# Projections into four PSUM banks until a layer's first scores, and gate projection z:0 moved ahead of the first merge

## The chip, the cores and the metric

One core of a Trainium2 chip runs the whole program. Its engines are PE (matmul; PEld loads its weights), DVE (vector), ACT (scalar functions), POOL (GpSimd) and SP, which here only issues transfers. The metric is the device time of one execution in microseconds, lower is better.

## The reference

Two decoder layers on a sequence of 256 with width 1024, in float32. Cut to what matters here:

```python
proj = x @ w_in                       # q, k, v of both mixers, gate z, decay logits
q_a, k_a, v_a, a_logit, b_logit, z, q_b, k_b, v_b = jnp.split(proj, offs, -1)
# group A: gated DeltaNet, 4 heads of 128, chunks of 64
qkv = jax.nn.silu(causal_dwconv(jnp.concatenate([q, k, v], -1), conv_w))   # width 4
sol = lax.linalg.triangular_solve(t_mat, rhs, left_side=True, lower=True, unit_diagonal=True)
o = o * lax.rsqrt(jnp.mean(o * o, -1, keepdims=True) + NORM_EPS) * norm_g
o = o * jax.nn.silu(z)
# group B: causal softmax attention with partial rotary on q and k, 8 heads of 64
mix = jnp.concatenate([o_a, o_b], -1) @ w_out
x = layer_norm(DEEPNORM_ALPHA * x + mix, ln1_g, ln1_b)
hid = causal_dwconv(x @ w_up, ffn_conv_w) + ffn_conv_b                     # width 3
ffn = (jax.nn.silu(gate) * val) @ w_down
x = layer_norm(DEEPNORM_ALPHA * x + ffn, ln2_g, ln2_b)
```

With 256 positions and blocks of 256 the block-sparse attention is plain causal attention.

## The kernel before

**Projections.** Activations lie transposed, 128 channels by 256 positions a tile. `proj` makes one projection of 128 channels: SP loads a weight chunk into `wr` (L181; ring of 6), ACT rounds it to a high part `wh` (L196) and DVE takes the residue `wl` (L197; on some chunks of the feed-forward part POOL does), both in rings of 5, and PE runs 24 matmuls: eight pairs for high weights with the high and low part of the input (L211, L212), then eight for the residues (L214). The result stands in one PSUM bank, which is read from there: a convolution unit (`ka`, `va`, `qa`) has ACT scale it into `cv` (L424), DVE add three shifted products (L427, each reading the bank), ACT take tanh (L429) and DVE the product (L430); a gate unit (`z`) has ACT take tanh (L441) and DVE the product (L442); a rotary unit (`qb`, `kb`) has ACT copy it (L447) and DVE shuffle and multiply (L449, L450).

**PSUM.** Eight banks: two called `pj` (projections), two called `mx` (scores, their transposes, products with the values and the last steps of the DeltaNet group), four called `ac` (small matrices, later the output projection). A tile taken from a group waits until the tile that held its bank before has been read for the last time.

**Mixer of a layer.** The DeltaNet group builds a matrix per head (`kk`, `decay`, `am`), writes it to DRAM, and POOL inverts its blocks of 16 (`solve`, L527 to L530). The inverse goes to DRAM (L531) and comes back spread over the partitions (L538). Unit `ex` expands it on DVE (L543), and the merges `lt` (L560), `lx` (L575, L581), `mt` (L596) and `mx` (L605, L607) join blocks to 32, 64 and 128. Here the "first merge" begins with `ex`. `zsol`, `az` and `o` apply it (L691, L697, L703), DVE normalizes the outputs (L711), and `ot` transposes them (L719). The attention group runs for each pair of heads `s` (scores L619 and mask L623 on PE, maximum L625 and L626 on DVE, exponential L633 on ACT), `tr` (transposes, L648 to L650) and `pv` (L662, L663). Each `s` and each `tr` takes both `mx` banks. `w` units begin the output projection (L732 to L734).

**Order.** `ORDER` lists the units of a layer. A unit's instructions are traced in that order, and a scheduler then places them on each engine, with priority by the order traced; an instruction may be placed earlier than its unit where its inputs are there in the scheduler's own model. Letters behind `@` forbid that: the unit's instructions on that engine (P for PE, A, D, G for POOL) stay behind the last ones of the unit before. At run time each engine follows its fixed order and waits on semaphores.

Of the kernel before, what the change touches and what calls it, by code (L numbers as in the profile page):

```python
# [22 lines left out]
D = 1024  # L23
S = 256
# [12 lines left out]
DP = 8 * (NB * 128 + NB)  # L37
# [33 lines left out]

ORDER = ("""
ab ka:0@A ab2@G ka:2@P qb:0@GP ka:3@G ka:1 kk:0 decay@AGD kk:1@PG kb:0@G kb:2@G sk@GP ld:0@P ld:1@DG kb:3@G am:0@A
vb:1@DAGP qb:1@GP kb:1@G rp@DG am:1@AG qb:2@G qb:3 va:2@GP va:0@G va:3 rk@G solve@G va:1@D qa:1 qa:0@P ex@DPA lt@GP s:0@DA lx@DAP
tr:0@AD mt:32:0@GAP mx:32:0@G mt:32:1@G vt:0@G rp@GP mx:32:1@PAG pv:0 mt:64:0@GDPA mt:64:1@AG s:1@AGD
qa:3@G qa:2@GP mx:64:0@PG tr:1@PA mx:64:1@D z:0 s:2@GADP pv:1@GA sq:0@DG vt:1@ADP zsol:0@D az tr:2@A s:3@GDP pv:2@AG
tr:3@PGD zsol:1@A z:2@G qk@GP sq:1@GDA o:0@ADP z:1@G wu:1@PGA pv:3@AGP o:1@GDP w:0:5 w:0:4@D w:1:4@PDA z:3@PD w:1:6@G
w:0:7@GD w:1:5@GPD ot:1@AP ot:0@G wu:0@PA w:0:6@A
""", """
vb:1@APDG ab@GD ka:0@G ab2@G ka:3 qb:0@P ka:2@G ka:1@P kk:0 decay@ADG kb:0 kk:1@GA kb:2 sk@AP kb:3@G kb:1@PG qb:2  # L80
rp@GPD qb:3@GP am:0@PA qb:1@DP am:1@AG ld:0@GP va:1@P va:0@GP rk@AG va:2@G ld:1@D solve@GP va:3@P qa:1 ex@D lt@DAP s:0@GD
lx@DAPG mt:32:0@A mt:32:1@AG vt:0@PD rp@GAD tr:0@AP qa:0 mx:32:0 pv:0@A mx:32:1@AD mt:64:0@AGD mt:64:1@DGP s:1@A
qa:3 qa:2@P mx:64:1@APD tr:1@P z:0@G s:2@G sq:0@D vt:1@DG mx:64:0@GDP pv:1 zsol:0@DGP az@A tr:2@DA s:3@GD pv:2@AG
tr:3@PDGA zsol:1@PD z:2 qk@PDG sq:1@G o:0@ADP z:1 pv:3@AGD o:1@A w:0:5@G w:0:4@DP w:1:4@GDA z:3@PA wu:0@DP w:1:6@GP
wu:1@GA w:0:7@D ot:1@D ot:0@AP w:1:5 w:0:6@PA
""")
# [3 lines left out]
def hybrid_kernel(ctx, tc, xT, x, wab, wch, par, lnrow, cst, msk, out):  # L90
# [22 lines left out]
    def ps_p():  # L113
        return ps_w()[:, 0:S]
# [4 lines left out]
    def ps_m():  # L119
        return mx.tile([128, 512], F32, name="mx")  # L120
# [217 lines left out]
    vb = vb_first()  # L338
    const_prep()

    for l in range(DEPTH):
# [79 lines left out]
        def gdn_conv(ps, ct, dst):  # L421
# [7 lines left out]
            act.activation(th, cv, AF.Tanh, scale=0.5)  # L429
            dve.scalar_tensor_tensor(dst, th, 1.0, cv, op0=OP.add, op1=OP.mult)  # L430

        def u_conv(c0, ct, dst, h):
            ps = ps_p()
            proj(ps, l, c0 + h)
            gdn_conv(ps, ct + h, dst[:, h, :])

        def u_z(h):
            ps = ps_p()
            proj(ps, l, C_Z + h)
            th = mt("th", [128, S], 2)  # L440
            act.activation(th, ps, AF.Tanh, scale=0.5)  # L441
            dve.scalar_tensor_tensor(zs[:, h, :], th, 1.0, ps, op0=OP.add, op1=OP.mult)  # L442

        def u_rope(c0, dst, p):
            ps = ps_p()
            proj(ps, l, c0 + p)
            act.activation(dst[:, p, :], ps, AF.Copy)  # L447
            sw = mt("sw", [128, S], N_SW)
            dve.stream_shuffle(sw, dst[:, p, :], [(i + 8) % 16 if i < 16 else i for i in range(32)])  # L449
            dve.tensor_tensor(dst[:, p, :], dst[:, p, :], ropec, op=OP.mult)  # L450
            st["rp"] = st.get("rp", []) + [(dst, p, sw)]
# [158 lines left out]
                    dve.tensor_copy(X[hi, b, :, 0:n], ps[hi])  # L610

        def u_s(p):
            sc = [ps_m() for _ in range(2)]
            mxv = small.tile([128, 4], F32, name="mxv")
            for js, ks in ((slice(0, 128), slice(0, 128)), (slice(128, 384), slice(0, S))):
                for a in range(2):
                    rs = slice(64 * a, 64 * a + 64)
                    qs = slice(js.start, js.start + 128)
                    pe.matmul(sc[a][:, js], qb[rs, p, qs], kb[rs, p, ks], start=js.start == 0, stop=False,  # L619
                              skip_group_check=True)  # L620
            for a in range(2):
                for i in (0, 256):
                    pe.matmul(sc[a][:, i:i + 128], ident_b, neg_lt, start=False, stop=i > 0, skip_group_check=True)  # L623
            for a in range(2):
                dve.tensor_reduce(mxv[:, a:a + 1], sc[a][:, 0:128], axis=AX.X, op=OP.max)  # L625
                dve.tensor_reduce(mxv[:, 2 + a:3 + a], sc[a][:, 128:384], axis=AX.X, op=OP.max)  # L626
            dve.tensor_scalar(mxv, mxv, -(DH ** -0.5), None, op0=OP.mult)
            P = [mt("P0", [128, 2, 128], 2), mt("P1", [128, 2, S], 2)]
            sv = small.tile([128, 4], F32, name="sv")
            for i, js in enumerate((slice(0, 128), slice(128, 384))):  # L630
                for a in range(2):
                    c = 2 * i + a
                    act.activation(P[i][:, a, :], sc[a][:, js], AF.Exp, scale=DH ** -0.5, bias=mxv[:, c:c + 1],  # L633
                                   accum_out=sv[:, c:c + 1])
            rv = small.tile([128, 4], F32, name="rv")
            dve.reciprocal(rv, sv)
            for i in range(2):
                for a in range(2):
                    c = 2 * i + a
                    dve.tensor_scalar(P[i][:, a, :], P[i][:, a, :], rv[:, c:c + 1], None, op0=OP.mult)  # L640
            st["P", p] = P
# [362 lines left out]
```

## Time and profile before

| | |
|---|---|
| three runs | 713.30, 714.86, 716.22 us; median 714.86 |
| profiled execution | 714.04 us, of which the span from first to last instruction is 712.3 |
| mean granted clock of PE | 0.984 |
| busy share of the span | PE 97%, DVE 81%, ACT 56%, POOL 28% |
| mixer of layer 0, of layer 1 | about 19 to 161 us, 367 to 512 us |

Busy time of PE counts pipelined matmuls from start to modelled end, so that short waits between them do not show. The granted clock is a share of 2.4 GHz; 0.50 is 1.2 GHz. Idle time of an engine is put down to the event that ended it.

### The profile page before, as it was taken

To read this page: it belongs to the slowest core of one execution; us is meant where nothing else is said; L and a number is where in the kernel's file an instruction comes from. 1 tells how busy PE (TensorE), PEld (TensorE's weight loads), DVE (VectorE), ACT (ScalarE), POOL (GpSimd) and SP (SyncE) were. 2 spreads that over 40 slices of the span, in tenths; PEclk is the share of its full clock that TensorE was granted. 3 is DMA by queue.
4 is the path that set the end of the run, shared out by engine and by line. 5 is a ranking of instruction groups with operands and counts; after the bars stand their busy time and mean duration, and the time that the engine had idled before them with its cause. 6 is when DMAs were issued, how large, how long until landed. Compare 5 with 4: busy or idle time off the path is not lost.

```text
span 712.3 us, 13664 instructions
## 1 busy us (share of the span) xinstructions
PE 688.6 (97%) x5056; PEld 618.6 (87%) x5056; DVE 576.9 (81%) x1273; ACT 400.8 (56%) x908; POOL 197.2 (28%) x200
## 2 busy tenths in 40 slices
PE   8989999999999999999999989999999999999994
PEld 5979888787999999999888988888789999999994
DVE  5899877599788887778879987776998888887756
ACT  5644466546666665656355445556476566666531
POOL 0045700013333343332002382000153333333413
PEclk9999999999999999999999997999999999999998
DMA  8876351521766665656153437134246766666201
GB/s 313 305 244 192 78 198 40 199 89 61 276 220 194 211 222 184 202 181 205 60 201 129 144 94 222 61 103 159 66 150 234 233 213 194 214 206 202 70 1 60
DMA packets 41217, 118.07 MB, mean 166 GB/s; under 512 B 10176, under 2 KB 12992, under 8 KB 40640
## 3 DMA queue, kind: packets, MB, share of 16 engines
q1 hardware_dynamic: 41152, 117.21, 49.6%
q8 instruction: 40, 0.66, 0.3%
q14 instruction: 25, 0.20, 0.1%
HBM read 114.84 MB, written 2.36 MB: 165 GB/s over the span
## 4 chain that ended last, share of the span: by engine, by line
PE 86%; DVE 9%; ACT 1%; issue 1%; DMA 1%; SPq 0%; DVEq 0%; ACTq 0%
PE pj L211 16%; PE pj L212 15%; PE pj L214 15%; PE ac L732 8%; PE ac L733 8%; PE ac L734 8%; DVE wl L197 3%; PE pj L225 1%; PE pj L222 1%; DVE cv L427 1%; PE mx L619 1%; PE pj L223 1%; PE mx L313 1%; DMA wr<-in_wch_dram 1%; PE mx L662 1%
## 5 line engine op out<-in xcount | busy, mean ns | idle before, releaser
L196 ACT ACTIVATE wh<-wr 128x512 fp32r<-128x512 f32 x376 | 219.5, 622 | 108.2 <-PE pj L212 49.1
L211 PE MATMUL pj<-xh,wh 128*128 128x256 f32 x1024 | 258.6, 289 | 7.4 <-DVE cv L427 7.4
L212 PE MATMUL pj<-xl,wh 128*128 128x256 f32 x1024 | 257.2, 287 | 0.0
L197 DVE TENSOR_TENSOR wl<-wr,wh 128x512 fp32r<-128x512 f32 x292 | 206.7, 736 | 28.2 <-ACT wh L196 14.7
L211 PEld LDWEIGHTS pj<-xh,wh 128*128 128x128 f32 x1024 | 198.6, 194 | 11.4 <-issue 5.4
L212 PEld LDWEIGHTS pj<-xl,wh 128*128 128x128 f32 x1024 | 199.1, 194 | 1.6
L197 POOL TENSOR_TENSOR wl<-wr,wh 128x512 fp32r<-128x512 f32 x84 | 116.2, 1405 | 204.9 <-ACT wh L196 199.7
L214 PE MATMUL pj<-xh,wl 128*128 128x256 f32 x1024 | 147.6, 286 | 0.0
L214 PEld LDWEIGHTS pj<-xh,wl 128*128 128x128 f32 x1024 | 134.2, 194 | 0.4 <-issue 0.2
L733 PE MATMUL ac<-wh,fal 128*128 128x512 f32 x144 | 56.4, 392 | 0.0
L732 PE MATMUL ac<-wh,fah 128*128 128x512 f32 x144 | 56.1, 392 | 0.0
L734 PE MATMUL ac<-wl,fah 128*128 128x512 f32 x144 | 56.0, 389 | 0.0
L842 DVE TENSOR_TENSOR fal<-fth,fah 128x256 fp32r<-128x256 f32 (+1 forms) x48 | 36.8, 767 | 17.3 <-ACT fah L841 17.0
L828 DVE SCALAR_TENSOR_TENSOR fc<-pj,par,fc 128x255 f32<-128x255 f32 x80 | 38.1, 476 | 4.2 <-ACT fc L824 2.8
L828 DVE SCALAR_TENSOR_TENSOR fc<-pj,hw,fc 128x255 f32<-128x255 f32 x80 | 38.3, 478 | 3.7 <-ACT fc L824 2.4
L817 POOL TENSOR_SCALAR hw<-par 128x66 f32<-128x66 f32 x2 | 2.1, 1048 | 139.2 <-DVE wlh L197 139.2
L839 DVE SCALAR_TENSOR_TENSOR fth<-fth,fc 128x256 f32<-128x256 f32 (+1 forms) x48 | 23.6, 492 | 20.1 <-ACT fth L838 20.1
L841 ACT ACTIVATE fah<-fth 128x256 fp32r<-128x256 f32 (+1 forms) x48 | 18.9, 393 | 34.8 <-DVE fth L840 34.8
L838 ACT ACTIVATE fth<-fc 128x256 f32<-128x256 f32 (+1 forms) x48 | 19.2, 400 | 31.7 <-DVE fc L828 31.5
L427 DVE SCALAR_TENSOR_TENSOR cv<-pj,par,cv 128x255 f32<-128x255 f32 (+2 forms) x72 | 33.8, 472 | 0.6 <-ACT cv L424 0.3
L734 PEld LDWEIGHTS ac<-wl,fah 128*128 128x128 f32 x144 | 27.1, 188 | 5.9
L732 PEld LDWEIGHTS ac<-wh,fah 128*128 128x128 f32 x144 | 27.1, 189 | 4.8
(257 smaller groups left out, 1030.5 us busy)
## 6 DMA issues: line engine op xcount, KB each, us to landing
wr<-in_wch_dram SPq DMA_DIRECT2D x195, 512.0 KB, 4.1
lnb<-in_lnrow_dram SPq DMA_DIRECT2D x4, 1024.0 KB, 4.6
xres<-in_x_dram SPq DMA_DIRECT2D x2, 512.0 KB, 6.8
da<-A SPq DMA_DIRECT2D x4, 256.0 KB, 3.4
ka<-in_wch_dram SPq DMA_DIRECT2D x2, 512.0 KB, 4.5
qa<-in_wch_dram SPq DMA_DIRECT2D x2, 512.0 KB, 5.1
qb<-in_wch_dram SPq DMA_DIRECT2D x2, 512.0 KB, 4.8
kb<-in_wch_dram SPq DMA_DIRECT2D x2, 512.0 KB, 5.7
```

Source lines behind the costliest of these rows:

```text
L196: ih = act.activation(h[:, s], raw[:, s], AF.Copy)
L197: il = le.tensor_tensor(lo[:, s], raw[:, s], h[:, s].bitcast(F32), op=OP.subtract)
L211: pe.matmul(ps, h[:, k, :], xh[:, k, :], start=k == 0, stop=False)
L212: pe.matmul(ps, h[:, k, :], xl[:, k, :], start=False, stop=False)
L214: pe.matmul(ps, lo[:, k, :], xh[:, k, :], start=False, stop=k == KT - 1)
L427: dve.scalar_tensor_tensor(cv[:, o:], ps[:, :S - o], w[:, j:j + 1], cv[:, o:], op0=OP.mult, op1=OP.add)
L732: pe.matmul(ps, a_h, w_h[:, ns], start=start and i == 0, stop=False, skip_group_check=True)
L733: pe.matmul(ps, a_l, w_h[:, ns], start=False, stop=False, skip_group_check=True)
L734: pe.matmul(ps, a_h, w_l[:, ns], start=False, stop=stop and i == len(items) - 1, skip_group_check=True)
L828: dve.scalar_tensor_tensor(cv[:, d], ps[:, d.start - o:d.stop - o], w[:, q:q + 1], cv[:, d], op0=OP.mult, op1=OP.add)
L839: dve.scalar_tensor_tensor(th, th, 1.0, cg[:, ts], op0=OP.add, op1=OP.mult)
L842: dve.tensor_tensor(al, th, ah.bitcast(F32), op=OP.subtract)
```

## The change

Until a layer's first scores unit has been traced, every other projection (the first, third and so on) takes an `mx` bank, the others a `pj` bank; behind it all take `pj` as before. And gate projection `z:0` moves in both layers from the stretch of the later merges to a place right ahead of `ex`.

```diff
--- before.py
+++ after.py
@@ -71,16 +71,16 @@
 
 ORDER = ("""
 ab ka:0@A ab2@G ka:2@P qb:0@GP ka:3@G ka:1 kk:0 decay@AGD kk:1@PG kb:0@G kb:2@G sk@GP ld:0@P ld:1@DG kb:3@G am:0@A
-vb:1@DAGP qb:1@GP kb:1@G rp@DG am:1@AG qb:2@G qb:3 va:2@GP va:0@G va:3 rk@G solve@G va:1@D qa:1 qa:0@P ex@DPA lt@GP s:0@DA lx@DAP
+vb:1@DAGP qb:1@GP kb:1@G rp@DG am:1@AG qb:2@G qb:3 va:2@GP va:0@G va:3 rk@G solve@G va:1@D qa:1 qa:0@P z:0 ex@DPA lt@GP s:0@DA lx@DAP
 tr:0@AD mt:32:0@GAP mx:32:0@G mt:32:1@G vt:0@G rp@GP mx:32:1@PAG pv:0 mt:64:0@GDPA mt:64:1@AG s:1@AGD
-qa:3@G qa:2@GP mx:64:0@PG tr:1@PA mx:64:1@D z:0 s:2@GADP pv:1@GA sq:0@DG vt:1@ADP zsol:0@D az tr:2@A s:3@GDP pv:2@AG
+qa:3@G qa:2@GP mx:64:0@PG tr:1@PA mx:64:1@D s:2@GADP pv:1@GA sq:0@DG vt:1@ADP zsol:0@D az tr:2@A s:3@GDP pv:2@AG
 tr:3@PGD zsol:1@A z:2@G qk@GP sq:1@GDA o:0@ADP z:1@G wu:1@PGA pv:3@AGP o:1@GDP w:0:5 w:0:4@D w:1:4@PDA z:3@PD w:1:6@G
 w:0:7@GD w:1:5@GPD ot:1@AP ot:0@G wu:0@PA w:0:6@A
 """, """
 vb:1@APDG ab@GD ka:0@G ab2@G ka:3 qb:0@P ka:2@G ka:1@P kk:0 decay@ADG kb:0 kk:1@GA kb:2 sk@AP kb:3@G kb:1@PG qb:2
-rp@GPD qb:3@GP am:0@PA qb:1@DP am:1@AG ld:0@GP va:1@P va:0@GP rk@AG va:2@G ld:1@D solve@GP va:3@P qa:1 ex@D lt@DAP s:0@GD
+rp@GPD qb:3@GP am:0@PA qb:1@DP am:1@AG ld:0@GP va:1@P va:0@GP rk@AG va:2@G ld:1@D solve@GP va:3@P qa:1 z:0 ex@D lt@DAP s:0@GD
 lx@DAPG mt:32:0@A mt:32:1@AG vt:0@PD rp@GAD tr:0@AP qa:0 mx:32:0 pv:0@A mx:32:1@AD mt:64:0@AGD mt:64:1@DGP s:1@A
-qa:3 qa:2@P mx:64:1@APD tr:1@P z:0@G s:2@G sq:0@D vt:1@DG mx:64:0@GDP pv:1 zsol:0@DGP az@A tr:2@DA s:3@GD pv:2@AG
+qa:3 qa:2@P mx:64:1@APD tr:1@P s:2@G sq:0@D vt:1@DG mx:64:0@GDP pv:1 zsol:0@DGP az@A tr:2@DA s:3@GD pv:2@AG
 tr:3@PDGA zsol:1@PD z:2 qk@PDG sq:1@G o:0@ADP z:1 pv:3@AGD o:1@A w:0:5@G w:0:4@DP w:1:4@GDA z:3@PA wu:0@DP w:1:6@GP
 wu:1@GA w:0:7@D ot:1@D ot:0@AP w:1:5 w:0:6@PA
 """)
@@ -429,20 +429,24 @@
             act.activation(th, cv, AF.Tanh, scale=0.5)
             dve.scalar_tensor_tensor(dst, th, 1.0, cv, op0=OP.add, op1=OP.mult)
 
+        def ps_q():
+            st["proj"] = st.get("proj", 0) + 1
+            return ps_m()[:, 0:S] if st["proj"] % 2 and "s" not in st else ps_p()
+
         def u_conv(c0, ct, dst, h):
-            ps = ps_p()
+            ps = ps_q()
             proj(ps, l, c0 + h)
             gdn_conv(ps, ct + h, dst[:, h, :])
 
         def u_z(h):
-            ps = ps_p()
+            ps = ps_q()
             proj(ps, l, C_Z + h)
             th = mt("th", [128, S], 2)
             act.activation(th, ps, AF.Tanh, scale=0.5)
             dve.scalar_tensor_tensor(zs[:, h, :], th, 1.0, ps, op0=OP.add, op1=OP.mult)
 
         def u_rope(c0, dst, p):
-            ps = ps_p()
+            ps = ps_q()
             proj(ps, l, c0 + p)
             act.activation(dst[:, p, :], ps, AF.Copy)
             sw = mt("sw", [128, S], N_SW)
@@ -610,6 +614,7 @@
                     dve.tensor_copy(X[hi, b, :, 0:n], ps[hi])
 
         def u_s(p):
+            st["s"] = True
             sc = [ps_m() for _ in range(2)]
             mxv = small.tile([128, 4], F32, name="mxv")
             for js, ks in ((slice(0, 128), slice(0, 128)), (slice(128, 384), slice(0, S))):
```

The projections of the output, of the feed-forward part and of the values (`vb`) do not go through `ps_q`. Nothing else differs.

## Rows read from the trace of the kernel before

**Rows 1.** The page, busy us (share of the span) x instructions of the engines.

```profile
PE 688.6 (97%) x5056; PEld 618.6 (87%) x5056; DVE 576.9 (81%) x1273; ACT 400.8 (56%) x908; POOL 197.2 (28%) x200
```

**Rows 2.** Waits of PE: line, releaser, us in total, times, longest.

```profile
PE pj L211 <- DVE cv L427: 7.4, 6, 2.1
```

**Rows 3.** PE's timeline at four gaps: start, us, instruction, idle before and releaser.

```profile
39.20 0.36 PE L211 MATMUL pj<-xh,wh 128*128 128x256 f32 x1 [1.37 <-DVE cv L427]
...
72.05 0.43 PE L211 MATMUL pj<-xh,wh 128*128 128x256 f32 x1 [2.08 <-DVE cv L427]
...
419.14 0.36 PE L211 MATMUL pj<-xh,wh 128*128 128x256 f32 x1 [2.04 <-DVE cv L427]
...
435.45 0.36 PE L211 MATMUL pj<-xh,wh 128*128 128x256 f32 x1 [1.48 <-DVE cv L427]
```

**Rows 4.** Windows: stretch, us, busy us of five engines, PEclk, DMA.

```profile
45.00:75.00 30.00, 27.92 (x216) 27.35 (x215) 29.55 (x80) 12.98 (x29) 17.01 (x22) 0.95 0.68 218
...
72.10:75.60 3.50, 3.50 (x17) 3.50 (x18) 2.69 (x6) 0.67 (x2) 2.87 (x9) 0.51 0.11 46
...
419.10:423.40 4.30, 4.26 (x24) 4.25 (x24) 2.80 (x6) 1.92 (x4) 3.56 (x10) 0.64 0.02 6
...
437.40:447.70 10.30, 10.30 (x142) 9.68 (x143) 6.85 (x22) 4.97 (x17) 0.00 (x0) 0.50 0.65 241
...
91.00:146.00 55.00, 54.68 (x583) 44.76 (x582) 39.17 (x121) 34.61 (x119) 0.00 (x0) 1.00 0.38 133
...
436.20:496.50 60.30, 60.11 (x599) 50.30 (x598) 41.53 (x125) 35.32 (x121) 0.00 (x0) 0.92 0.40 137
```

**Rows 5.** The chain that ended last, in order of time: start, us, what.

```profile
51.73 0.96 PE pj L214 x8
...
54.61 0.96 PE pj L214 x8
...
145.98 0.88 PE mx L719 x8
...
496.64 0.87 PE mx L719 x8
```

**Rows 6.** DVE's timeline, layer 0, projections and first merge.

```profile
66.24 1.88 DVE L197 TENSOR_TENSOR wl<-wr,wh 128x512 fp32r<-128x512 f32 x3
...
69.92 0.47 DVE L427 SCALAR_TENSOR_TENSOR cv<-pj,par,cv 128x255 f32<-128x255 f32 x1
...
70.92 0.98 DVE L427 SCALAR_TENSOR_TENSOR cv<-pj,par,cv 128x254 f32<-128x254 f32 x2
...
76.75 0.77 DVE L197 TENSOR_TENSOR wl<-wr,wh 128x512 fp32r<-128x512 f32 x1 [1.92 <-PE pj L214]
...
90.64 0.42 DVE L430 SCALAR_TENSOR_TENSOR qa<-th,cv 128x256 f32<-128x256 f32 x1 [0.91 <-ACT th L429]
...
90.98 0.42 DVE L543 TENSOR_TENSOR gX<-PT,kt 128x256 f32<-128x256 f32 x1
```

**Rows 7.** SP's timeline at the load for the merge, and its landing.

```profile
85.32 0.38 SPq L538 DMA_DIRECT2D PT<-dx  x1
...
432.32 0.38 SPq L538 DMA_DIRECT2D PT<-dx  x1
...
DMA to landing us min/median/max: 3.2/3.3/3.3
```

**Rows 8.** One line, L442: count, ns min/median/max, first and last start.

```profile
L442 DVE SCALAR_TENSOR_TENSOR zs<-th,pj x8: 407/412/420, 111.4 to 495.1; 128x256 f32<-128x256 f32 x8
```

**Rows 9.** DVE's timeline, layer 1, ahead of the first merge.

```profile
430.20 3.00 DVE L197 TENSOR_TENSOR wl<-wr,wh 128x512 fp32r<-128x512 f32 x1
...
436.19 0.42 DVE L543 TENSOR_TENSOR gX<-PT,kt 128x256 f32<-128x256 f32 x1
```

**Rows 10.** Layer 0 behind the merge: DVE's timeline, and PE's groups in 91:146.

```profile
143.91 0.68 DVE L711 SCALAR_TENSOR_TENSOR T<-mx,rsz 128x512 f32<-128x512 f32 x1
...
L214 PE MATMUL pj<-xh,wl 128*128 128x256 f32 x40 | 6.3, 291 | 0.0
```

## Prediction

> **What bounds the kernel now.** I read the page first: PE is busy 97% of the span [rows 1], so a gain can only come from stretches in which PE stands still or runs at its lower clock. The waits by engine come next. One group leads on PE: the first matmul of a projection waits for the last convolution instruction on DVE, 7.4 us in all, 6 times [rows 2]. That is a wait for a bank: a projection writes one of the two `pj` banks, and its bank comes free when L427 has read it for the last time. PE's timeline places the four longest, two in each layer's run of projections or just behind it: 1.37 us at 39.2, 2.08 at 72.1, 2.04 at 419.1, 1.48 at 435.5 [rows 3]. The other two share the remaining 0.4.
>
> The windows show a second cost. Behind three of the gaps the granted clock is near half, so at 1.2 GHz, for part or all of a stretch: 0.51 over 72.1 to 75.6, 0.64 over 419.1 to 423.4, 0.50 over 437.4 to 447.7 [rows 4]. At most that cost 3.5 x 0.49 + 4.3 x 0.36 + 10.3 x 0.50 = 1.7 + 1.5 + 5.2 = 8.4 us. Gaps and clock together are 15.8 us: the ceiling of what banks can give back.
>
> Why is DVE late? Its timeline at 66 to 77 tells [rows 6]. It makes three weight residues in a row (66.24), and only at 69.92 starts the first convolution, which ends at 71.9, where PE restarts. But at 76.75 DVE itself has waited 1.92 us for PE to give up a weight buffer: its residues were so far ahead that the ring was full. So DVE's work was in a poor order for PE, not too much; weights stood ready throughout the gap. Yet DVE has little room: 29.55 of 30 us are busy in 45 to 75 [rows 4]. A projection is 2.88 us on PE at full clock (51.73 to 54.61, [rows 5]).
>
> Last, the question that decides the sum: does the end of a layer follow PE's time in the projections? The first merge (L543, unit `ex`) starts at 90.98 and at 436.19 [rows 6, 9]. It needs the inverse blocks that POOL computes, written to DRAM and read back; the read is issued at 85.32 and 432.32 and lands 3.3 us later, at 88.6 and 435.6 [rows 7]. Neither POOL nor this load is touched by the change. PE can run ahead of the merge, but the merge cannot follow by more.
>
> **The change, part by part.**
>
> *Four banks until the first scores.* No instruction is added: the odd projections of a layer write an `mx` bank instead. PE may run two projections, 2 x 2.88 = 5.8 us, further ahead of DVE. The longest gap was 2.08, so I expect the gaps at 72.1 and 419.1, the two short ones, and the clock loss behind the long ones to go. For PE that is 2.1 + 2.0 + 0.4 + 1.7 + 1.5 = 7.7 us. The gap at 39.2 lies where DVE is the full engine, so I bound it by 0 and 1.4 and count 0.
>
> *What of that reaches the merge, layer 0.* The merge can start at 88.6 by the load. By DVE: before it DVE idled 1.92 and 0.91 us [rows 6], and z:0's gate product (0.41 us, [rows 8]) is new ahead of it: 90.98 - 2.83 + 0.41 = 88.6. Both say 2.4 us at best. The bounds are 0 (DVE's idle stays, since its order is fixed when the program is built) and 2.4; I take 1.8, nearer the upper end, since the larger idle piece was the full weight ring behind the gap that goes.
>
> *Layer 1.* Here the load says 435.6 against 436.19: 0.6 us at best, I take 0.5. The 3.5 us that PE wins at 419.1 cannot move the merge. They are PE work done ahead, which thins out what stands beside the merge.
>
> *The merge at full clock, layer 1.* From the merge to the transposes of the outputs (L719), layer 0 takes 145.98 - 90.98 = 55.0 us at clock 1.00 and layer 1 496.64 - 436.19 = 60.4 us at clock 0.92 [rows 4 to 6, 9]. If the clock stays up, layer 1 comes to layer 0's figure: 5.4 us. What would keep it up: the 1.48 us gap that stands before the fall goes, and z:0 gives PE 2.88 us of full matmuls just ahead of the merge. Bounds: 0 (the clock falls anyway) and the 1.5 + 5.2 of gap and clock; I take 5.3. One thing of that gap stays: it followed a residue that took 3.00 us on DVE [rows 9], against 0.77 for its like [rows 6]; with four banks PE covers 5.8 us of such lateness.
>
> *z:0 earlier.* Its 24 matmuls, splits, weight load and gate product are moved, not removed. Behind the merge PE loses 2.88 us of filler. In that stretch PE is busy 54.68 of 55 us [rows 4], but the scores, their transposes, the products and the merge's last steps follow each other there through two `mx` banks. The last of them, L711, starts at 143.91 and ends 0.68 later, 1.4 us before the transposes that need it [rows 5, 10]. So the chain is only that much shorter than PE's work, and 2.88 us less on PE is worth 0 to 1.4. I count 0. Its load goes to SP's queue ahead of the loads of qa:3 and qa:2, which move back by one; none was waited for in the gaps. Cost 0, covered by the full ring; without that cover PE would wait for a load.
>
> *The new wait.* s:0 needs both `mx` banks, and now two projections hold them: qa:1 and z:0 in layer 0, va:2 and qa:1 in layer 1. PE takes its instructions in order, so behind a waiting s:0 stand the next projection and the merge's first matmuls (L560). In the old order the score matmuls were free to fill. Below, it costs nothing, since DVE is forced to reduce the scores after the merge anyway; above, it costs what DVE's lateness cost at 72.1, 2.08 us a layer. I take 0, since PE is some 3.5 us ahead there and would otherwise wait for the merge; the upper end goes into the range.
>
> **Sum.** 1.8 + 0.5 + 5.3 = 7.6 us. The profiled execution took 714.04 us (span 712.3 and 1.7 around it): 706.4. The runs shown have a median 0.8 above it, so I predict 707.0.
>
> **The rivals.**
>
> *PE alone decides (E).* If the end followed PE's time everywhere, all 15.8 us come back: 698 to 702. For it: PE's 97%. Against it: the merge waits for a load that doesn't move.
>
> *The clock still falls in layer 1's merge (B).* PE arrives early, has used up qa:0, qa:3 and z:0, and stands still until 435.6 plus the expansion. Then only 1.8 + 0.5 remains: 711.7, from 709.5 to 713.5. For it: this stretch is mostly small matmuls, and the fall came just at its start. Against it: layer 0 went through the same stretch at 1.00.
>
> *The waits change their name (C).* More banks don't make DVE faster. With DVE at 98% of 45 to 75 the lateness may come back as waits of PE for residues, or of s:0 for its two banks at 2.08 a layer: 7.6 - 2 x 2.08 - the clock that such gaps cost (1.5 to 1.7 a layer) leaves 0.2: 714, from 712 to 717. The Trainium skill has such a case: in "TensorE: Matmul & The Clock Gate", section "HAM oscillation — how this bites in real kernels", PSUM double-buffering on top of a better loop order gave no further gain. By that the sum would be 0 here; the full weight ring in this trace speaks against it, as the banks and not the weights held PE.
>
> *Slower (D).* Layer 0's merge loses its clock. In 91 to 146 PE ends five projections now (40 of the matmuls that close one, eight each, [rows 10]); with z:0 and most of qa:2 done before, some three are left as filler. If PE then idles between the small matmuls and the clock falls from 91 on, layer 0 pays what layer 1 paid, 5.4 us per 10 us at half clock, and layer 1 keeps paying: 714.0 - 2.3 + 5.4 = 717; a fall twice as long gives 722. It decides for slower once it costs layer 0 more than 2.3 us. For it: layer 1 shows the state can hold for 10.3 us. Against it: PE had hardly any idle there, and the other gate projections may be drawn forward. The Trainium skill names such a state on the same page, in "A second HAM failure mode: psum-queue depth-cycling": idle moments between groups that cycle through banks bring the clock down and up again. By that rule D's 717 to 722 would be the result; in this trace layer 0's merge stayed at 1.00.
>
> **How the numbers follow.** The sum (A) 0.45, 704 to 709.5; B 0.20; C 0.14; D 0.13; E 0.08. Half a per cent, 3.6 us, is about what this kernel's runs can tell from no change: faster is below 711.3, slower above 718.4. Faster: A, E and 0.07 of B, 0.60. Slower: most of D and a little of C, 0.13. Within: 0.27. The range reaches from 701.5 (E's faster half out) to 716.0 (D and C's end out), which leaves about 0.18; the likeliest case alone is 704 to 709.5.
>
> **What would show it.** In the trace after, PE's wait L211 on L427 falls from 7.4 to under 1 us; no clock below 0.9 before the merge in either layer; L543 starts about 1.8 us earlier against its layer's start in layer 0 and 0.5 in layer 1; layer 1's merge to L719 is 55 to 56 us at clock 0.99 or more. B shows as a stretch at 0.50 behind layer 1's L543. C shows as PE idle at L214 for L197, or at L619 for L442 or L427, of 2 us or more. D shows as a clock below 0.9 in layer 0 between the merge and L719. What would make me wrong above all: the program's fixed order on each engine is made anew at build time, and a new order can put a convolution or a score behind something late that no row here shows.

## The result: slower, and the profile after

The kernel after takes 724.36 us (median of 4 runs, 723.77 to 724.87), beside 714.62 for the kernel before on the same chip: a ratio of 1.0127, 95% interval 1.0098 to 1.0155. The forecast was 707.0, with a range up to 716.0, so it is wrong in sign and in range. The profiled execution took 724.75 us with a span of 722.9 and a mean granted clock of 0.974 (before 712.3 and 0.984). In the lines after, the numbers moved by four or five: `ex` is L547 (was L543), the merge's first product L564 (L560), the scores L624 (L619), the gate's tanh and product L445 and L446 (L441, L442), the outputs' normalization L716 (L711), their transposes L724 (L719), SP's write and read of the solve's result L535 and L542 (L531, L538).

The old wait is gone. These are PE's waits after, in the columns of [rows 2]:

```profile
PE ac L564 <- DVE gX L547: 5.5, 1, 5.5
PE mx L624 <- DVE zs L446: 4.1, 1, 4.1
PE mx L624 <- DVE cv L427: 3.0, 2, 1.8
...
PE ac L737 <- ACT oh L727: 1.4, 1, 1.4
```

L211 on L427, 7.4 us in [rows 2], is no longer there, and 12.6 us stand under two new names: the merge's first product waits for `ex`, and the first scores wait for a bank. The fourth line, the output projection waiting for the outputs, is new too. PE's timeline says where they lie:

```profile
83.73 0.89 PE L624 MATMUL mx<-kb,qb 64*128 64x128 f32 x4 [1.77 <-DVE cv L427]
...
92.12 0.79 PE L624 MATMUL mx<-kb,qb 64*128 64x128 f32 x2 [4.11 <-DVE zs L446]
...
437.40 0.89 PE L624 MATMUL mx<-kb,qb 64*128 64x128 f32 x4 [1.20 <-DVE cv L427]
...
444.60 1.07 PE L564 MATMUL ac<-gX,A 64*64 64x32 f32 x16 [5.46 <-DVE gX L547]
```

All stand just ahead of a merge, and the clock falls there. Windows after, in the columns of [rows 4] (us, busy of PE, PEld, DVE, ACT, POOL, then clock):

```profile
45.00:75.00 30.00, 30.00 (x253) 30.00 (x252) 29.20 (x75) 14.22 (x32) 16.25 (x20) 1.00 0.62 184
...
92.00:102.20 10.20, 10.08 (x148) 8.55 (x149) 4.18 (x12) 4.69 (x16) 0.00 (x0) 0.50 0.57 229
102.30:152.00 49.70, 49.52 (x435) 40.44 (x435) 34.79 (x109) 31.15 (x103) 0.00 (x0) 1.00 0.32 107
440.20:457.10 16.90, 12.50 (x162) 11.82 (x163) 8.31 (x23) 6.30 (x20) 0.00 (x0) 0.50 0.62 214
```

The projections run as forecast: PE dense over 45 to 75 (27.92 of 30 us in [rows 4]) at full clock. But layer 0's merge, at 1.00 before, has 10.2 us at 0.50, which is 1.2 GHz, and layer 1's low stretch is 16.9 us instead of 10.3. The merge's start is later, not earlier. ACT's and DVE's timelines ahead of it, each with layer 0 and then layer 1:

```profile
89.02 1.15 ACT L196 ACTIVATE wh<-wr 128x512 fp32r<-128x512 f32 x2 [4.99 <-DMA wr<-in_wch_dram]
90.86 0.42 ACT L429 ACTIVATE th<-cv 128x256 f32<-128x256 f32 x1 [0.69 <-DVE cv L427]
91.18 0.36 ACT L445 ACTIVATE th<-mx 128x256 f32<-128x256 f32 x1
...
441.97 1.15 ACT L196 ACTIVATE wh<-wr 128x512 fp32r<-128x512 f32 x2 [6.98 <-DMA wr<-in_wch_dram]
```

```profile
89.68 0.69 DVE L197 TENSOR_TENSOR wl<-wr,wh 128x512 fp32r<-128x512 f32 x1 [1.73 <-ACT wh L196]
...
91.65 0.41 DVE L446 SCALAR_TENSOR_TENSOR zs<-th,mx 128x256 f32<-128x256 f32 x1
91.98 0.42 DVE L547 TENSOR_TENSOR gX<-PT,kt 128x256 f32<-128x256 f32 x1
...
442.63 0.69 DVE L197 TENSOR_TENSOR wl<-wr,wh 128x512 fp32r<-128x512 f32 x1 [5.38 <-ACT wh L196]
443.45 0.43 DVE L430 SCALAR_TENSOR_TENSOR qa<-th,cv 128x256 f32<-128x256 f32 x1
443.80 0.41 DVE L446 SCALAR_TENSOR_TENSOR zs<-th,pj 128x256 f32<-128x256 f32 x1
444.13 0.42 DVE L547 TENSOR_TENSOR gX<-PT,kt 128x256 f32<-128x256 f32 x1
```

ACT stands 4.99 and 6.98 us on a weight load, for a split that PE needs only four chunks later. Behind it in ACT's fixed order is z:0's tanh, behind that on DVE z:0's product, which frees the bank of the scores, and `ex`. Why the load is late, SP's timeline shows:

```profile
61.72 7.78 SPq L181 DMA_DIRECT2D wr<-in_wch_dram  x3
83.95 0.60 SPq L535 DMA_DIRECT2D dx<-P  x1
84.68 0.51 SPq L181 DMA_DIRECT2D wr<-in_wch_dram  x1
```

SP issues no weight load between 69.5 and 84.7: the next thing in its order is the write of POOL's solve (L535), which waits for POOL, and the loads wait behind it. In the kernel before the queue stood in the same way (L531 at 82.88 and 429.90). In layer 0 nobody asked for that load yet. In layer 1 ACT already stood for it, but without z:0's tanh behind it:

```profile
434.43 0.63 ACT L196 ACTIVATE wh<-wr 128x512 fp32r<-128x512 f32 x1 [3.44 <-DMA wr<-in_wch_dram]
```

### The profile page after: what moved, and what is told of

It reads as the page before. It is cut to its first block, busy times and chain, and to the rows that moved or that the text cites. A ratio compares the mean times of both kernels' runs of the same rounds, so it can differ in the third digit from the quotient of the medians.

```text
span 722.9 us, 13658 instructions
## 1 busy us (share of the span) xinstructions
PE 692.3 (96%) x5056; PEld 621.6 (86%) x5056; DVE 576.6 (80%) x1273; ACT 401.6 (56%) x908; POOL 198.5 (27%) x200
## 4 chain that ended last, share of the span: by engine, by line
PE 80%; DVE 7%; POOL 5%; DMA 4%; ACT 2%; issue 2%; SPq 1%; DVEq 0%; ACTq 0%; POOLq 0%
PE pj L214 13%; PE pj L211 13%; PE pj L212 13%; PE ac L738 8%; PE ac L737 8%; PE ac L739 8%; POOL P L533 2%; POOL T L531 2%; DMA wr<-in_wch_dram 2%; DVE wl L197 2%; PE mx L624 1%; PE pj L225 1%; ACT wh L196 1%; PE mx L313 1%; PE pj L222 1%
## 5 line engine op out<-in xcount | busy, mean ns | idle before, releaser
L211 PE MATMUL pj<-xh,wh 128*128 128x256 f32 x872 | 220.6, 289 | 0.0
L212 PE MATMUL pj<-xl,wh 128*128 128x256 f32 x872 | 219.4, 287 | 0.0
L211 PEld LDWEIGHTS pj<-xh,wh 128*128 128x128 f32 x872 | 170.3, 195 | 2.0 <-issue 0.3
L212 PEld LDWEIGHTS pj<-xl,wh 128*128 128x128 f32 x872 | 170.2, 195 | 1.6
L214 PE MATMUL pj<-xh,wl 128*128 128x256 f32 x872 | 126.8, 287 | 0.0
L214 PEld LDWEIGHTS pj<-xh,wl 128*128 128x128 f32 x872 | 114.7, 194 | 0.3
L737 PE MATMUL ac<-wh,fah 128*128 128x512 f32 x144 | 56.1, 392 | 0.0
L211 PE MATMUL mx<-xh,wh 128*128 128x256 f32 x152 | 38.2, 287 | 0.0
L212 PE MATMUL mx<-xl,wh 128*128 128x256 f32 x152 | 37.8, 285 | 0.0
```

What stands on the lines that cost most here:

```text
L211: pe.matmul(ps, h[:, k, :], xh[:, k, :], start=k == 0, stop=False)
L212: pe.matmul(ps, h[:, k, :], xl[:, k, :], start=False, stop=False)
L214: pe.matmul(ps, lo[:, k, :], xh[:, k, :], start=False, stop=k == KT - 1)
L737: pe.matmul(ps, a_h, w_h[:, ns], start=start and i == 0, stop=False, skip_group_check=True)
```

## The experiments

I split each profiled execution at the same events, the start of `ex` and the first transpose of the outputs (`ot`, L719 or L724); layer 1 is counted from its first L222. "Half" is PE's time at half clock between the event that the column names and `ot`. Us, starts read from the timelines; each ratio is to runs of the kernel before on the same chip, whose medians lay between 714.62 and 715.97. Layer 0's starts count from the first instruction, so they carry whatever came before: e2, e5 and e15 have 3.4 us at half clock at 40 us, where the kernel before has none, and the residue that waits for a buffer at 76.75 in the kernel before does so at 78.29 in e2. The letters of the theories in the forecasts below are their own: theories B, C and D are not the prediction's cases B, C and D.

| kernel | median | ratio (95%) | L0 `ex` | L0 `ex` to `ot` | L1 to `ex` | L1 `ex` to `ot` | half after `ex`, L0 / L1 |
|---|---|---|---|---|---|---|---|
| before | 714.62 | 1 | 90.98 | 54.84 | 81.81 | 60.29 | 0 / 10.2 |
| after | 724.36 | 1.0127 (1.0098, 1.0155) | 91.98 | 61.05 | 82.66 | 61.12 | 10.2 / 13.1 |
| e1 banks alone | 715.39 | 1.0003 (0.9981, 1.0026) | 89.80 | 55.13 | 82.03 | 61.08 | 0 / 10.7 |
| e2 z:0 alone | 720.04 | 1.0056 (1.0024, 1.0088) | 92.76 | 57.47 | 83.31 | 60.37 | 0 / 10.2 |
| e4 hold | 721.99 | 1.0090 (1.0071, 1.0110) | 89.53 | 62.57 | 81.62 | 61.74 | 12.9 / 11.8 |
| e12 limit, hold | 720.15 | 1.0076 (1.0049, 1.0102) | 90.07 | 58.16 | 81.85 | 61.31 | 0 / 10.2 |
| e15 z:0 alone, residues back | 716.70 | 1.0015 (0.9999, 1.0030) | 94.35 | 54.76 | 83.07 | 60.38 | 0 / 10.2 |
| e16 limit, hold, residues back | 714.96 | 0.9997 (0.9970, 1.0024) | 90.99 | 53.50 | 82.00 | 61.25 | 0 / 10.2 |

**The two halves.** e1 takes the change's ORDER back and keeps the banks; e2 keeps the ORDER and takes the banks back.

```diff
 e1, layer 0 (layer 1 alike):  -... qa:0@P z:0 ex@DPA ...    +... qa:0@P ex@DPA ... (z:0 again behind mx:64:1)
 e2:  -            ps = ps_q()                   +            ps = ps_p()
```

> The four banks alone: the projections take their banks in turn from the two pools as in the kernel after, and the order of the units is that of the kernel before, so z:0 stays in the merge's stretch. Theory Q (SyncE's queue is in order; with PE early, ScalarE comes to a weight split whose load is behind the issue that waits for GpSimd's solve, and tanh and everything behind it stand until that load lands): the banks by themselves are enough for it, so ScalarE waits 3 to 7 us for a weight load next to the solve's end in both layers, the merges run at half clock, and the time is 716 to 724. Theory B (the banks of the first scores, held by the last two projections): qa:0 is the last projection and lies in a projection bank, so the scores find their banks free and the time is 709 to 713. Theory F (z:0 is missing as filler in the merge): the filler is back, 707 to 712.

> z:0 ahead of the merge alone: the order of the units is that of the kernel after, and the projections stay in their two banks. Theory Q: PE waits for its bank as before, so ScalarE is never ahead of the loads and no wait for a load comes up; the time is 713 to 718, by what the merge loses without z:0. Theory B: the scores' banks are free, as before; 711 to 716. Theory F: z:0 is missing in both merges, they fall to half clock as in the kernel after, and the time is 720 to 726.

The banks alone are worth nothing, 1.0003, which no theory had; z:0 alone costs 0.56%. B, F and Q all missed the time of e1. Q's mark came true there all the same: ACT stands 4.42 us on a load in layer 0 and 6.88 in layer 1 (first row below), and the time does not change, so such a stand alone costs nothing that e1 can show. In e2, where Q expected none, ACT stands 6.00 us in layer 1. What the banks do is in e1's waits and its window:

```profile
434.36 0.63 ACT L196 ACTIVATE wh<-wr 128x512 fp32r<-128x512 f32 x1 [6.88 <-DMA wr<-in_wch_dram]
...
PE ac L564 <- DVE gX L547: 5.4, 2, 4.6
PE mx L624 <- DVE cv L427: 3.3, 2, 2.0
...
45.00:75.00 30.00, 30.00 (x252) 30.00 (x251) 29.76 (x78) 14.42 (x32) 16.79 (x21) 1.00 0.61 188
...
89.80 0.42 DVE L547 TENSOR_TENSOR gX<-PT,kt 128x256 f32<-128x256 f32 x1 [0.18 <-DMA PT<-dx]
```

PE is early and waits at the merge instead. `ex` gains 1.2 us in layer 0 (I had 1.8), and then DVE waits for the load of the solve's result. In layer 1 it gains nothing. e2 has F's time, but not by F's way: its layer 0 merge stays at full clock.

**The queue.** e3 moves the write and the read of the solve's result to POOL's queue, e4 leaves the queue alone and keeps the blocked split behind z:0.

```diff
 e3  -            dma.dma_start(dap(dx, ...            +            se.dma_start(dap(dx, ...
     -            dma.dma_start(xc.rearrange(...       +            se.dma_start(xc.rearrange(...
 e4  +                d = late[e] if late["n"] == 5 and e in late else hold.get(e)
     +                if d: tc.add_manual_dep(i.ins, d.name, ...      # fifth chunk behind z:0, on ACT and DVE
```

> The kernel after with the issue that writes the solve's result and the one that reads it back on GpSimd's queue in place of SyncE's; nothing else is edited. Theory Q: no weight load stands behind the solve any more, ScalarE's waits of 4.99 and 6.98 us for a load go to under 1 us, and with them the waits of PE ahead of the merges; the time is 706 to 714, if GpSimd's own issue and landing are not slower by more than 1 us each. Theory B and theory F: the waits of PE keep their length under other names and the time stays at 722 to 726.

> The kernel after with one ordering more in each layer: the two splits (ScalarE and VectorE) of the fifth weight chunk behind z:0 stay behind z:0's tanh and its product on these engines. SyncE's queue is as in the kernel after. Theory Q: tanh of qa:0 and of z:0 come as soon as their inputs are there, some 4 us earlier in layer 0 and 7 us in layer 1, z:0's bank comes free before the scores need it, and the time is 710 to 717. Theory B: the scores still need both banks and z:0 still holds one, PE waits over 3 us at the first scores, 721 to 725. Theory F: 722 to 726.

e3 took 728.44 us, 1.0185 (1.0159, 1.0211). ACT no longer waits for a load ahead of layer 0's merge (its longest wait in the last 12 us is 1.31 us, for 4.99), but POOL issued the read 5.0 us behind the write (87.07 and 92.08; SP 83.95 and 86.39), and `ex` came at 95.86. The remedy costs more than the illness and settles nothing about the price. e4 does: `ex` comes 2.4 us earlier in layer 0 and 1.0 in layer 1, and the time falls by 2.4 us. So Q's stand is a quarter of the loss in this kernel, where z:0's steps are behind it. The time lies in B's range and not in Q's, B's mark is still there, and the clock still falls:

```profile
88.96 0.41 DVE L446 SCALAR_TENSOR_TENSOR zs<-th,mx 128x256 f32<-128x256 f32 x1
89.53 0.43 DVE L547 TENSOR_TENSOR gX<-PT,kt 128x256 f32<-128x256 f32 x1
...
89.43 1.65 PE L624 MATMUL mx<-kb,qb 64*128 64x128 f32 x4 [3.64 <-DVE zs L446]
```

**What sets the merge's start.** e1 suggested the solve. e5, e6 and e7 cut it to 3 of 14 steps (in the kernel before, in e1's and in the kernel after); e9 leaves out one of three convolution taps on DVE in the kernel after; e10 and e13 do both. All of these leave work out.

```diff
 e5 to e7, e10   -for c in range(1, NB - 1):   +for c in range(1, 4):     (e13: range(1, 5))
 e9, e10, e13    -for j in (2, 1, 0):          +for j in (2, 1):
```

> The kernel before with GpSimd's solve cut: it runs 3 of its 14 steps, so the inverse is left incomplete and the output is not the reference's; the solve's span of 17 us falls by about 9 in each layer. Theory S (the merge starts when the chain through VectorE's last A0, GpSimd's solve and two small transfers is done, and PE's time ahead of that is free): the merge can start earlier, but only until PE, which in this kernel still waits for its two banks, sets the start; it gains 2 to 4 us a layer and comes to 705 to 711. Rival P (PE sets the start of the merge in this kernel already): 713 to 716.

> The four banks alone (order of the units as before), with the same cut of the solve; the output is not the reference's. Theory S: what the banks bring ahead of the merge, some 5 us a layer, is now on the path; the time is 692 to 702 and at least 4 us below the kernel before with the same cut. Rival P and theory B (PE's waits at the scores' banks are what eats the gain): no more than 2 us below the kernel before with the same cut.

> The kernel after with the same cut of the solve; the output is not the reference's. Theories S and C (C: PE stands ahead of the merge because z:0 is done and the solve is not, and the clock falls into the merge for it): PE no longer runs dry ahead of the merge, the half clock in layer 0's merge is gone, the stretch from the first L564 to the last product of the outputs is 48 to 50 us in layer 0 where it was 52.6, and the time is within 4 us of the four banks alone with the same cut. Theory F (z:0 is missing as filler in the merge, whenever that starts): the stretch stays at 52 us or more and the time is 6 to 10 us over that of the four banks alone with the cut.

> The kernel after with one of the three taps left out on VectorE in each of the twelve convolutions of a layer (the output is not the reference's); ten of them stand ahead of the merge, so VectorE has about 10 x 0.41 = 4.1 us less to do there in each layer. Theory D (two bounds set the merge's start, within 2 us of one another in layer 0: VectorE's own queue, and the chain through GpSimd's solve; PE's time is neither): the first L547 of layer 0 comes 1 to 3 us earlier and then waits for the solve's result, layer 1 gains less than 1.5 us, where the solve is the later one; 719 to 723. Theory S alone (the solve is the only bound): no earlier start in either layer, 722 to 725.

> Both cuts at once, the tap left out on VectorE and 3 of the solve's 14 steps, in the kernel after (the output is not the reference's). With the solve's cut alone the first L547 of layer 0 still started at 90.1 us, with VectorE busy without a gap in the 50 us ahead of it. Theory D: with both bounds moved the merge starts at 85 to 87.5 us in layer 0 and some 3 us earlier in layer 1 too, and the time is 704 to 710, 5 us or more below the solve's cut alone (715.4). Theory S alone: within 2.5 us of 715.4.

> Both cuts in the kernel after once more (the tap left out on VectorE, and 4 of the solve's 14 steps; the output is not the reference's), now with layer 1's small load L379 ahead of the solve's issue on SyncE's queue, where the run with 3 steps had it behind and VectorE stood 6.55 us for it. Theory D: without that stand the first L547 of layer 0 starts at 85 to 88 us (90.1 with the solve's cut alone, where VectorE had no gap), and the time is 706 to 713. Theory S alone: 90 us or later, 714 to 718. Theory Q: some other weight load behind the solve's issue makes ScalarE, and behind it VectorE, stand again for more than 3 us in the 20 us ahead of the merge, and the start is at 89 to 92.

| kernel | median | ratio (95%) | L0 `ex` | L0 `ex` to `ot` | L1 to `ex` | L1 `ex` to `ot` |
|---|---|---|---|---|---|---|
| e5 before, solve cut | 708.15 | 0.9911 (0.9876, 0.9946) | 92.30 | 54.83 | 80.01 | 56.24 |
| e6 banks alone, solve cut | 713.41 | 0.9976 (0.9951, 1.0000) | 92.13 | 55.49 | 78.36 | 58.77 |
| e7 after, solve cut | 715.43 | 1.0013 (0.9989, 1.0037) | 90.13 | 57.94 | 78.39 | 60.20 |
| e9 after, a tap less | 721.42 | 1.0089 (1.0060, 1.0118) | 90.84 | 59.71 | 82.75 | 61.64 |
| e10 after, both | 716.67 | 1.0023 (1.0001, 1.0044) | 91.68 | 59.20 | 77.53 | 62.63 |
| e13 after, both | 709.31 | 0.9932 (0.9902, 0.9961) | 86.37 | 57.75 | 77.31 | 61.13 |

e6 fells theory S: the banks stay worthless with the solve cut. POOL's part ends 8 to 11 us earlier in all of e5 to e7, yet layer 0's `ex` does not move below 90 us. In e7 DVE's window tells why, with the row of `ex` behind it:

```profile
40.00:90.10 50.10, 46.55 (x360) 45.06 (x360) 49.81 (x121) 24.75 (x54) 19.95 (x22) 0.97 0.65 204
...
90.13 0.42 DVE L547 TENSOR_TENSOR gX<-PT,kt 128x256 f32<-128x256 f32 x1
```

DVE is busy 49.81 of the 50.10 us and in its timeline has no gap over 0.1 us in the 50 us ahead of `ex`. So I formed D: two bounds lie within 2 us of one another, DVE's own queue and the solve. One cut alone moves the start by 1.1 (e9) and 1.9 us (e7), both by 5.6 (e13), which is more than their sum. That is how two bounds side by side look, and PE is neither of them. But neither single cut shows a bound cleanly. e4, which cuts nothing, moves the start by 2.4 us, more than e7. And e9 was not held by the read, as theory D had it (issued at 86.34, landed by 90.0, `ex` at 90.84): ACT stood on the load behind L535, so the solve's end also holds the merge by way of SP's queue. That the read can be the bound shows where DVE waits for it, 0.18 us in e1's layer 0 and 2.58 in e12's layer 1. e9's row on ACT and e12's on DVE:

```profile
88.67 1.15 ACT L196 ACTIVATE wh<-wr 128x512 fp32r<-128x512 f32 x2 [5.38 <-DMA wr<-in_wch_dram]
...
441.31 0.42 DVE L547 TENSOR_TENSOR gX<-PT,kt 128x256 f32<-128x256 f32 x1 [2.58 <-DMA PT<-dx]
```

e10 missed because the scheduler had put layer 1's small load (L379) behind L535 on SP's queue, Q's mechanism by accident. Its rows on SP and ACT:

```profile
72.52 0.60 SPq L535 DMA_DIRECT2D dx<-P  x1
73.22 0.54 SPq L181 DMA_DIRECT2D wr<-in_wch_dram  x1
73.81 0.43 SPq L379 DMA_DIRECT2D abr<-in_wab_dram  x1
...
77.40 0.26 ACT L381 ACTIVATE abw<-abr 128x64 fp32r<-128x64 f32 x1 [8.01 <-DMA abr<-in_wab_dram]
```

DVE stood 6.55 us for ACT there; 91.68 less 6.55 is 85.1, and e13, with that load ahead, has 86.37.

e7 speaks on the clock too: with z:0 ahead of the merge, but PE's last stand (2.31 us at L624) over at 86.35 and its half clock over at 90.67, layer 0's merge has its full clock, as theory C said, and from L564 to the last product of `o` with E0 (L708, L703 before) it takes 49.24 us (52.63 after, 48.49 before). F falls for that stretch.

**The scores' banks, and other orders.** e8 lends the pool of the scores to the first sixteen projections only, e12 adds e4's ordering, e14 is e1 with e8's limit, e11 is e14 with qa:0 and qa:3 moved ahead of layer 1's L564.

```diff
 e8, e11, e12, e14   -if st["proj"] % 2 and "s" not in st else    +if st["proj"] % 2 and st["proj"] < 17 else
 e11, layer 1        -qa:1 ex@D lt@DAP s:0@GD                     +qa:1 qa:0 ex@D qa:3 lt@P s:0@GD
```

> The kernel after with the pool of the scores lent only to the first sixteen projections of a layer, so that the last three (z:0 among them) lie in the two projection banks and the first scores find both of theirs free. Theory B: the waits of the first scores (4.1 us for z:0's product, 3.0 us for the last step of a convolution) go, and the time is 716 to 720. Theories S and C: the scores come some us earlier, but the transposed product L564 waits for the solve's result as late as before, PE runs dry for as long in sum, and the time is 721 to 726.

> The four banks without z:0 moved, the pool of the scores lent to the first sixteen projections only, and in layer 1 qa:0 and qa:3 (another projection, which the kernel after has behind the merge's first products) ordered ahead of the first L564, so that PE has 3 us more to do while it would stand for the solve. Theory C (the half clock of layer 1's merge comes from PE's stand ahead of it and costs some 5 us): the half clock in layer 1's merge is gone or shorter, and the time is 709 to 713. Against it: VectorE gets qa:3's splits and evictions ahead of the merge, some 2.5 us, as it got z:0's; then 715 to 719.

> The kernel after with both of the earlier edits: the pool of the scores lent to the first sixteen projections only, and the splits of the fifth chunk behind z:0 held back behind z:0's tanh and product. Both new waits that the trace showed are then gone. Theory D: z:0's own work on VectorE and the missing filler stay; 719 to 722, still slower than before by some 5 us. Theories Q and B together (the two waits are the whole loss): 712 to 716.

> The four banks without z:0 moved, the pool of the scores lent to the first sixteen projections only: the best of the edits without z:0, tried as a version that could beat the kernel before. Theory D: nothing that sets the merge's start is touched, 713 to 717. Theory B: PE's 3.3 us at the first scores go, and with them the half clock in layer 1's merge; 707 to 711.

e8: 722.73 us, 1.0121 (1.0077, 1.0166). The waits of the first scores go, and the time is still in the range of theories S and C, not in B's. Layer 0's merge is back at full clock (57.84 us for 61.05), but L211 waits for L427 again (5.9 us in all) and L564 still waits 3.6 us. The profiled execution, the longest of the four at 725.18 us, has 6.8 us at half clock behind layer 0's `ot` and 17.1 in layer 1's merge, which takes 64.34 us. So B alone is worth little in time. e14: 716.45, 1.0013 (0.9996, 1.0031), nothing. e11: 726.72, 1.0157 (1.0128, 1.0186), far outside what I gave it on either side: `ex` of layer 1 comes at 86.6 us of its layer, and 27.3 us at half clock begin just ahead of it. With one more projection in front of the merge ACT stands 6.99 and then 1.64 us on loads (437.20 and 440.66): Q's stand again, with more behind it. e12 removes both new waits and is left at 720.15, where z:0 alone is (720.04); 6.8 us of half clock begin there at 149.95, behind `ot`.

**Where the rest of z:0's price is.** In e2 layer 0's merge is longer by 2.6 us at full clock. DVE's timeline at the last normalization shows it:

```profile
143.67 0.16 DVE L708 SCALAR_TENSOR_TENSOR wv<-so,sq 128x4 f32<-128x4 f32 x1 [1.73 <-ACT scr L706]
...
145.51 0.68 DVE L197 TENSOR_TENSOR wlh<-qb,whh 128x512 fp32r<-128x512 f32 x1
146.19 0.68 DVE L197 TENSOR_TENSOR wlh<-qb,whh 128x512 fp32r<-128x512 f32 x1
146.86 0.69 DVE L197 TENSOR_TENSOR wlh<-kb,whh 128x512 fp32r<-128x512 f32 x1
147.53 0.69 DVE L197 TENSOR_TENSOR wlh<-kb,whh 128x512 fp32r<-128x512 f32 x1
148.21 0.69 DVE L197 TENSOR_TENSOR wlh<-ka,whh 128x512 fp32r<-128x512 f32 x1
...
149.49 0.69 DVE L711 SCALAR_TENSOR_TENSOR T<-mx,rsz 128x512 f32<-128x512 f32 x1
```

The normalization is a chain of steps of 0.16 us; five residues for the feed-forward part stand between them. L708 to L711 takes 5.82 us; in the kernel before, L708 starts at 140.93 and L711 at 143.91 [rows 10], 2.98 us, with no such residue:

```profile
140.93 0.17 DVE L708 SCALAR_TENSOR_TENSOR wv<-so,sq 128x4 f32<-128x4 f32 x1 [0.81 <-ACT scr L706]
```

The kernel after has the same five rows and 5.82 us (146.47 to 152.29), and PE has done its output products by then and waits 1.43 us at L737. e15 and e16 hold these residues behind the normalization, in e2's kernel and in e12's:

```diff
+            outs[0] = dve.scalar_tensor_tensor(on, ps, 0.5 * f_, ...
+            hp is not None and outs and tc.add_manual_dep(il.ins, outs[0].ins.name, nosync, reason="outputs first")
```

> z:0 ahead of the merge alone, as before, with one ordering more: VectorE's residues of the weights held for the feed-forward part stay behind the normalization of the last outputs (L711). In the run without it five of them stood between the small steps of that normalization in layer 0, which took 5.82 us from L708 to L711 where the kernel before takes 2.98. Theory R (z:0's price at the end of layer 0's merge is that the scheduler, with less PE work there, draws later work forward into VectorE's chain): from L708 to L711 it is 3 to 4 us, the transposes of the outputs come 1.5 to 3 us earlier, and the time is 716 to 718.5. Against it (the residues have to be made anyway, and then PE waits for them): 719 to 721.

> The kernel after with the three edits together: the scores' banks free, the fifth chunk's splits behind z:0, the feed-forward residues behind the normalization of the outputs. Theory R: 717 to 719, some 2 us below the run with the first two. Against it: 719.5 to 721.

In e15's timeline the same two rows are 2.95 us apart:

```profile
145.30 0.16 DVE L708 SCALAR_TENSOR_TENSOR wv<-so,sq 128x4 f32<-128x4 f32 x1 [1.72 <-ACT scr L706]
148.25 0.69 DVE L711 SCALAR_TENSOR_TENSOR T<-mx,rsz 128x512 f32<-128x512 f32 x1
```

e15 (716.70, 1.0015) lies in theory R's range, e16 (714.96, 0.9997) below it. e15's gain is one of medians: its profiled execution is the longest of its twelve, 720.01 us beside e2's 720.22, with a merge 2.7 us shorter in layer 0 but an `ex` 1.6 us later. With the three side effects undone, the change costs and brings nothing that can be measured. The kernel before with its residues held back was not run, so whether that ordering gains there too is not shown. No version beat the kernel before; those under it (e5, e6, e13) leave work out.

## Why the prediction was wrong, point by point

**The reading of the bounds held in the main.** That PE's time isn't what the merge follows, that the load and DVE bound it at about 88.6 us, was nearly right: e1 gained 1.2 us for my 1.8, 0 for 0.5 in layer 1. The rest of PE's 7.7 us came back as waits at L564 and L624. I had that as "PE work done ahead" and counted it as harmless. "Neither POOL nor this load is touched" was off by 1.1 us: from its first step on POOL to its write the solve takes 17.9 us after (66.10 to 83.95) for 16.8 (66.06 to 82.88), and the read is issued at 86.39 for 85.32 (86.16 in e1). No run shows why.

**The term that carried the sum failed.** "The merge at full clock, layer 1", 5.3 us of 7.6, measured -0.8 (60.29 to 61.12); even e16 has 10.2 us at half clock there. Its size was nearly right: e5, the one kernel with that merge wholly at full clock, takes 56.24 us, 4.1 less. But I tied the clock to a 1.48 us gap and let an earlier PE remove it. An earlier PE stands longer (5.46 us at 444.60), since what it waits for hasn't moved. Case B names this and I gave it 0.20. Why layer 1 falls in nearly every kernel, also in e7 where PE waits less, is not settled. In e5 PE has no wait in the 15 us ahead of that merge, which would fit; but e6 keeps its clock from a stand of 1.75 us (433.91) until 450.75. e5's merge of layer 1, in the columns of [rows 4]:

```profile
435.70:492.00 56.30, 56.17 (x600) 46.53 (x600) 41.53 (x125) 35.38 (x121) 0.00 (x0) 1.00 0.33 111
```

**Case D came true, at 0.13, for a reason that I had not priced.** Layer 0's merge went to half clock for 10.2 us, and from L564 to the last product of `o` it took 52.63 us for 48.49, 4.1 more. I saw D as a lack of filler inside the merge. e2, e7 and e12 have that lack and keep the full clock; the kernel after, e3, e4 and e9, which fall, have PE standing 4.11, 4.87, 3.64 and 5.19 us right ahead of that merge. A stand that long isn't needed, though: e10 falls after 1.32 us at L624, e13 for 6.8 us after 1.54, and e14's profiled execution after 1.23 us of a wait for a bank inside the merge. D's sentence from the Trainium skill ("TensorE: Matmul & The Clock Gate", "A second HAM failure mode: psum-queue depth-cycling") gave the right side of the forecast; what goes with the fall in most of these traces is the stand, not a cycling of banks. The other sentence of the Trainium skill that I set aside (the same page, "HAM oscillation — how this bites in real kernels": in one kernel PSUM double-buffering gave no further gain) agrees with e1, 1.0003; the full weight ring that I held against it did not decide.

**"The new wait: I take 0" failed with its reason.** I argued that PE would otherwise wait for the merge anyway. In time that is nearly so (e8, 722.73). But while it waits at L624 nothing else runs, neither the next projection nor L564, and the clock falls over the merge that follows.

**"Its load: cost 0, covered by the full ring" failed.** I named the cover and the price without it, "PE would wait for a load"; it was ACT that waited, 4.99 and 6.98 us. I looked at the order of loads among themselves and not at L535 in the same queue, which waits for POOL. In layer 0 being early is what takes the cover away. In layer 1 it wasn't there: "none was waited for in the gaps" overlooked ACT's 3.44 us at 434.43 in the kernel before, a wait that ends inside the gap before 435.45. e4 prices it at 2.4 us, e4's edit and e8's together (e12) at 4.2.

**z:0's gate product, 0.41 us, was too small, and "count 0" behind the merge had the wrong sign.** With z:0 come two residues of 0.68 on DVE as well, 1.8 us in all by their lengths, on the queue that theory D has as a bound. How much of that reaches `ex` no run shows cleanly: e2's layer 0 was 1.5 us late before z:0 came, and its layer 1, where `ex` is 1.5 us later against its layer, also has ACT's 6.00 us on a load. Behind the merge I bounded the gain by 0 and 1.4. The mechanism is there: with the residues held back e16's layer 0 merge is 1.3 us shorter (53.50 for 54.84). What turned it into 2.6 us of loss in e2 is what the prediction's last sentence feared, the order made anew: the scheduler drew residues of the next stage into DVE's chain. The new order is in the traces; that it came of PE having less work there is not shown. e15 shows it by medians, 720.04 to 716.70.

So the sum is, by medians: two new waits, 724.36 to 720.15, 4.2 us; residues in the chain, with the half clock behind `ot` that goes with them, 720.15 to 714.96, 5.2 us (3.3 between e2 and e15); what is left is 0.3 us above the 714.62 of the kernel before. By the ratios, each to the kernel before on its own chip, the two steps are about 3.6 and 5.6 us. That the clock in layer 0's merge is part of the first 4.2 follows from the traces of e12 and e16, which have none of it; I did not change the clock by itself.

**Still open.** e6 is 5.3 us slower than e5 by the medians. Its trace shows ACT standing 4.35 us with a split that waits for PE to give up a buffer, and qa:0's tanh behind it, but no run priced that.

## What to carry to other kernels

Before giving an engine room to run ahead, ask what it will wait for then: if that doesn't move, the wait is only renamed, and on PE it can cost the clock of the stage behind. A split, a load or a residue that is issued early is free only while everything behind it in its queue has time, so read each in-order queue (SP's with its waiting write, ACT's, DVE's) from the item that will now come early. And where a scheduler remakes the order, compare the order of every engine in the stretch that lost work, not only in the one that gained it.

## What the runs showed that I had not expected

The same program can fall to half clock or not from one execution to the next. e14's profiled execution has 20.5 us at half clock in layer 0's merge and took 724.29 us; the other 12 of that kernel lie between 715.28 and 719.28, at a mean granted clock of 0.983 to 0.988 for its 0.969. For this kernel a single profile may thus miss the median by 8 us.

The small write of the solve's result took longer from POOL's queue than from SP's. In e3 the read is issued 5.0 us behind the write, of which POOL waited 4.18 us for the write to land; on SP the two issues are 2.4 us apart.

```profile
92.08 1.18 POOL L542 DMA_DIRECT2D PT<-dx  x1 [4.18 <-DMA dx<-P]
```

Just behind the solve POOL makes four products for the rotary units (L455, L456), and often the DVE instruction beside them takes 2.5 to 3.9 us in place of 0.4 to 0.8. The 3.00 us of [rows 9] is one; the kernel after has one of 3.33 us in layer 0 (83.89), where the kernel before has 1.00 us at 83.18 and POOL the longer times. e2 and e15 show both outcomes in layer 0, and with that most of the 1.6 us between their `ex`. DVE and POOL, e2 and then e15:

```profile
84.72 1.00 DVE L197 TENSOR_TENSOR wl<-wr,wh 128x512 fp32r<-128x512 f32 x1
84.36 1.95 POOL L455 TENSOR_TENSOR sw<-sw,kt 128x256 f32<-128x256 f32 x2
...
84.35 3.27 DVE L197 TENSOR_TENSOR wl<-wr,wh 128x512 fp32r<-128x512 f32 x1
84.26 1.41 POOL L455 TENSOR_TENSOR sw<-sw,kt 128x256 f32<-128x256 f32 x2
```
